# An encoder trunk on one core: the gate's activation table loaded in the last projection, and a down block's weight rounding behind the last pair's evictions

## Chip, cores and metric

The kernel runs on one core of a Trainium2 chip. The metric is the device time of the program in microseconds, the median of several runs. Engines are called as the profile calls them: PE (TensorE), DVE (VectorE), ACT (ScalarE), POOL (GpSimd) and SP (SyncE, which here only issues DMAs).

## Reference

A trunk of two layers over 512 tokens of width 1024, all in float32. Each layer has three token mixers side by side, gates that merge them, a last projection `w_o` with residual, a SwiGLU feed-forward stage of width 2816 and a gated input embedding.

```python
for i in range(DEPTH):                                   # DEPTH = 2
    h = rmsnorm(x, norm_mix[i])
    ...                                                  # three mixers: ya, yb, yc
    ga, gb, gc = jnp.split(jax.nn.sigmoid(gates), 3, axis=-1)
    merged = ga*(ya @ w_br_a[i]) + gb*(yb @ w_br_b[i]) + gc*(yc @ w_br_c[i])
    x = x + merged @ w_o[i]
    h = rmsnorm(x, norm_ffn[i])
    x = x + (jax.nn.silu(h @ w_ffn_gate[i]) * (h @ w_ffn_up[i])) @ w_ffn_down[i]
    h = rmsnorm(x, norm_ple[i])
    x = x + jax.nn.sigmoid(h @ w_ple_gate[i]) * (p[i] @ w_ple_in[i])
return rmsnorm(x, norm_final)
```

## The kernel before

**A product.** Activations stay on chip, transposed (features on the 128 partitions, 512 tokens along the free axis). Every float32 operand is split into a rounded high part and a low remainder, and a product is three matmuls: high·high, high·low, low·high (`mm3`). For weights, SP loads a raw tile `wr` by DMA, ACT rounds it into `wh` (a Copy activation: "the rounding"), and DVE subtracts for `wl` ("the low part"). `wr`, `wh` and `wl` have three buffers each. PSUM has three banks `mm`, two `sc`, two `tr` and one `av`. In traces a tile carries the name of the stage that made it: `ffn_wh`, `wo_x`, `mergeb_wr`.

**The order.** PE executes its matmuls in the order in which the code writes them. The other engines' instructions are placed by a list scheduler, by dependencies and priorities: `high_priority` lifts weight work ahead of what is written around it, and `behind(i, then)` orders instruction `i` after `then` on the same engine without a semaphore. Each engine then runs its queue in order, so an instruction that waits holds all behind it.

**ACT's tables.** ACT holds one set of function tables at a time; a change of set is an instruction of its own, `ACT_TABLE_LOAD`, which the build puts ahead of the first activation that needs another set. `act(..., table=...)` orders activations so that functions of different sets aren't mixed. Both programs hold 13 such loads.

**Stages of a layer.** Mixers, gates, two merge stages (the second, `mergeb`, multiplies by eight blocks of `w_br_b`, one about every 2.7 us), then `w_o`: eight output blocks, each with residual, the operands for the next norm and, in `quarters`, differences of activations t1 to t4 for the feed-forward stage. Then `ffn`, then `ple`.

**The feed-forward stage.** The 22 blocks of 128 gate and up columns are worked off in three parts of 8, 7 and 7 (`PARTS`). For one block, `seven` computes gate and up together as a 2×2 block product with seven instead of eight multiplications (Strassen-Winograd). Its weights are a11, a12 (one `wr` tile), a22 (`kh` and `a`), and the sums s1 to s4: s1, s2 are summed by POOL's accumulating DMAs into `qk` and rounded into `wh`; s3, s4 are summed on DVE into the last `qk` tile and rounded into a spare pair of tiles, `pt` for even blocks and `y` for odd ones. Three PSUM accumulators C, A and Q collect the products: three `mm` banks for an even block, `sc`, `sc`, `av` for an odd one. Evictions (ACT Copy, DVE add) bring them into `t` tiles; PE writes A once more, with s4, after A was evicted for s2. Products with 128x512 operands are L1005 and L1006 (odd blocks), with 128x256 operands L1008 to L1010 (even blocks). `rest`, flushed a little later, applies SiLU on ACT, multiplies by up on DVE and splits the result into a mid. Two blocks are interleaved (`sevens_of`). The s3 sum of each layer's block 2 is placed behind the split of block 0's mid (`self.held`), so block 0's SiLU stands ahead of it.

After each part come eight down blocks, each a sum over the part's mids. The first two run as a `pair`: all mids but the last for both, then the last mid for both, since the last block's SiLU is still to come; then `gemm` for the other six.

The lines of before that matter most are L143 (every activation), L157 (every two-operand DVE instruction), L171 (a weight tile's DMA), L177 to L179 (`mm3`), L908 (the residual's DMA in `w_o`), L1005 to L1010 (`product`). In the changed kernel the lines behind L162 are two higher, those of `seven` three.

Of the kernel before, what the change touches and what calls it, by code (L numbers as in the profile page):

```python
# [14 lines left out]
AF = mybir.ActivationFunctionType  # L15
# [5 lines left out]
P = 128  # L21
# [40 lines left out]
class Net:  # L62
# [96 lines left out]
    def stt(self, out, a, s, b, op0, op1):  # L159
        return self.nc.vector.scalar_tensor_tensor(out, a, s, b, op0, op1)  # L160

    def split(self, hi, lo, src):  # L162
        self.act(hi, src, AF.Copy)
        return self.tt(lo, src, hi.bitcast(F32), ALU.subtract)

    def weights(self, ap, n):
        with self.tc.high_priority(offset=min(self.w_ahead, self.tc.cur_priority - self.p0)):
            raw = self.sb("wr", [P, 1024])
            hi = self.sb("wh", [P, 1024], F32R)
            lo = self.sb("wl", [P, 1024], F32R)  # L170
            self.nc.sync.dma_start(raw[:, :n], ap[:, :n])  # L171
            self.low = self.split(hi[:, :n], lo[:, :n], raw[:, :n])
        return hi, lo

    def mm3(self, out, wh, wl, ah, al, first, last, **kw):
# [15 lines left out]
                         first and o + k == 0, last and o + k == n - 1)  # L191
                self.chunk()

    def pair(self, outs, aps, acts):


        n = len(acts)
        ws = [self.weights(ap, n * P) for ap in aps]
        for ks in (range(n - 1), (n - 1,)):
            for out, (wh, wl) in zip(outs, ws):  # L200
                for k in ks:
                    s = slice(k * P, (k + 1) * P)
                    self.mm3(out, wh[:, s], wl[:, s], *self.halves(acts[k]), k == 0, k == n - 1)
                    self.chunk()
# [695 lines left out]
    def w_o(self, mg, xsrc):  # L900
        self.phase = "wo"
        xs, h, st, self.four = [], [], [], []
        self.zs = [self.parts_of("z", [2, 256], 2, F32R) for _ in range(4)]
        for m in range(KD):
            if m % 2 == 0:
                two = self.parts_of("x", [512], 2)
            xo = two[m % 2]
            self.nc.sync.dma_start(xo, xsrc[m])  # L908
            if m == 0:
                both = [self.ps("mm") for _ in range(2)]  # L910
                self.pair(both, self.a["w_o"][self.i, 0:2], mg)
            if m < 2:
                ps = both[m]
            else:
                ps = self.ps("mm")
                self.gemm(ps, self.a["w_o"][self.i, m], mg)
            self.tt(xo, xo, ps, ALU.add)
            h.append(self.norm_chunk(m, xo, self.par(self.i, "ffn", m), "h", st, 512 if m % 2 else 256))
            xs.append(xo)
            if m == 4:  # L920
                self.mark = self.low_x
            if m in QUARTERS:
                self.four.append(self.quarters(xs, h, QUARTERS.index(m)))
        self.four.append(self.quarters(xs, h, 3))
        self.main_norm(st[0])
        return xs, h
# [31 lines left out]
    def seven(self, wg, wu, bs, tags, spare, md, first, fb, early, twice):  # L958
# [3 lines left out]
        with self.tc.high_priority(offset=min(self.w_ahead, self.tc.cur_priority - self.p0)):  # L962
            lo, up = slice(0, 512), slice(512, 1024)
# [10 lines left out]
            ws = {}  # L974

            def halve(hi, lo, src, names):
                i = self.split(hi, lo, src)
                for q, name in enumerate(names):
                    c = slice(q * 512, q * 512 + 512)
                    ws[name] = (hi[:, c], lo[:, c])  # L980
                return i

            wide = lambda: (self.sb("wh", [P, 1024], F32R), self.sb("wl", [P, 1024], F32R))
            i = halve(*wide(), g, ("a11", "a12"))
# [4 lines left out]
            i = self.tt(s3, s1, a22, ALU.add)  # L989
# [6 lines left out]
        C, A, Q = (self.ps(t, shape) for t in tags)  # L996

        def product(out, w, b, first=False):
            wh, wl = ws[w]
            mm = nc.tensor.matmul  # L1000
            for k in range(4):
                c = slice(k * P, k * P + P)
                both = bs[k][b]
                if len(out.shape) > 2:
                    mm(out, wh[:, c], both, start=first and k == 0, stop=False, skip_group_check=True)  # L1005
                    mm(out[:, 0], wl[:, c], both[:, 0], start=False, stop=k == 3, skip_group_check=True)  # L1006
                    continue
                mm(out, wh[:, c], both[:, 0], start=first and k == 0, stop=False, skip_group_check=True)  # L1008
                mm(out, wh[:, c], both[:, 1], start=False, stop=False, skip_group_check=True)  # L1009
                mm(out, wl[:, c], both[:, 0], start=False, stop=k == 3, skip_group_check=True)  # L1010
            self.chunk2()

        gg, uu = self.sb("t", [P, 2, 256]), self.sb("t", [P, 2, 256])
# [24 lines left out]
        product(A, "s2", "t1")  # L1038
        if twice:
            self.act(uu[:, 1], A[:, 0], AF.Copy)  # L1040
            self.act(gg[:, 0], A[:, 1], AF.Copy)
        else:
            self.act(uu[:, 1], A, AF.Copy)
        product(Q, "a22", "t4")
        if twice:
            self.tt(uu[:, 1], uu[:, 1], gg[:, 0], ALU.add)
# [32 lines left out]
    def sevens_of(self, pairs, head):  # L1079


        def go(*gens):
            for g in gens:
                next(g, None)
# [8 lines left out]
            one = two  # L1093
        go(one, one)

    def behind(self, i, then):

        self.tc.add_manual_dep(
            i.ins, then.ins.name,
            mybir.DependencyInfo(mybir.DependencyClass.NoSync, mybir.DependencyReason.DATA),  # L1100
            reason="order",
        )
# [12 lines left out]
    def ffn(self, h, x):  # L1115
        self.phase = "ffn"
        i = self.i
        self.halfs, self.pending = 0, []
        st, hn, bs = [], [], self.four
        spare = [[self.sb(t, [P, 1024], F32R) for _ in range(2)] for t in ("pt", "y")]  # L1120
        md8 = [self.sb(t, [P, 2, 512], F32R) for t in ["v"] * 3 + ["z"] + ["y"] * 3]
        md8.append(tuple(self.sb("e", [P, 512], F32R) for _ in range(2)))
        self.sums, self.sevens = [t for _ in range(2) for t in self.parts_of("qk", [1024], 2)], 0
        for part in PARTS:
            mids = md8[:len(part)]
            self.sevens_of((self.seven(self.a["w_fg"][i, fb], self.a["w_fu"][i, fb], bs,
                                       (("mm", "mm", "mm"), ("sc", "sc", "av"))[fb % 2],
                                       spare[fb % 2], md8[f], part[0] and f < 2, fb, fb == 0,
                                       fb % 2 == 1)
                            for f, fb in enumerate(part)), part[0] == 0)  # L1130
            self.flush()
            down = [self.a["w_fd"][i, m][:, part[0] * P:(part[-1] + 1) * P] for m in range(KD)]
            two = [self.ps(("mm", "sc")[part[-1] % 2 == 0]) for _ in range(2)]
            self.pair(two, down[:2], mids)
            for m in range(KD):
                if m < 2:
                    ps = two[m]
                else:
                    ps = self.ps("mm")
                    self.gemm(ps, down[m], mids)  # L1140
                d = self.sb("t", [P, 512])
                self.tt(d, ps, self.rb, ALU.mult)
                self.tt(x[m], x[m], d, ALU.subtract)
                if part is PARTS[-1]:
                    if m in (0, 2):
                        qk = self.parts_of("qk", [2, 512], 2, F32R)
                    hn.append(self.norm_chunk(m, x[m], self.par(i, "ple", m),
                                              qk[m % 2] if m < 4 else "z", st))
        self.main_norm(st[0])
        return hn  # L1150
# [109 lines left out]
    def final(self, h, x, pairs, hn, most):  # L1260
# [54 lines left out]
        def store(t):  # L1315
# [11 lines left out]
            nc.sync.dma_start(out[:, c], r[:, c])  # L1327

        pair, low, pgs, vs, columns, summed = [], [], [], [], [], []
        places = ("av", "mm", "av", "sc")  # L1330
        def inputs(t):
# [167 lines left out]
```

## Time and profile before

| | |
|---|---|
| median of 3 runs | 1768.84 us (1768.34 to 1769.42) |
| the profiled execution | 1768.67 us; its span 1766.9 us, 1.8 us lie around it |
| PE busy | 1757.0 us, 99% of the span, 9618 matmuls |
| DVE, ACT busy | 1387.4 us (79%), 934.6 us (53%) |
| granted TensorE clock | 1.0 throughout |
| DMA | 253.90 MB, mean 144 GB/s |

Starts are microseconds from the span's start, and the second number of a timeline row is the duration. Matmuls overlap, so a row's start and the start of the row behind it tell how long PE took, not its duration. The bracket at the end of a row is the engine's idle time ahead of it and the instruction whose end released it. "x2" stands for two instructions in a row of the same kind. The chain of work that ended last is followed back from the last instruction: a row of ACT or DVE in it is a time in which PE waited for that engine. The first layer's feed-forward stage begins at about 490 us, the second's at about 1365.

### The profile page before, as it was taken

What the parts mean: (1) busy time and instruction counts of PE and PEld (TensorE: products, weight loads), DVE (VectorE), ACT (ScalarE), POOL (GpSimd) and SP (SyncE); (2) the same over time, 40 slices, a digit from 0 to 9 for tenths busy, and PEclk for the clock granted to TensorE, in tenths of its full rate; (3) what the DMA queues carried; (4) which work ended last, traced back from release to release, by engine and by line L of the source; (5) the groups of instructions that cost most, each with busy time, mean ns of one, the idle gap of its engine ahead of it and who ended that gap; (6) DMA issues with size and microseconds to landing.
All of it is one profiled execution on the core that took longest, in us unless ns stands there. A gap on an engine that the chain in (4) does not pass through costs nothing.

```text
span 1766.9 us, 26211 instructions
## 1 busy us (share of the span) xinstructions
PE 1757.0 (99%) x9618; PEld 1525.0 (86%) x9618; DVE 1387.4 (79%) x2264; ACT 934.6 (53%) x1647; POOL 103.9 (6%) x114
## 2 busy tenths in 40 slices
PE   9999999999999999999999999999999999999998
PEld 7889888888899898898888888888888998989987
DVE  7967988998788676787776789789887875877776
ACT  5566555325576264464545655552356753645554
POOL 0000000000121010100000000000001210101000
PEclk9999999999999999999999999999999999999999
DMA  6565641334767365543446655322356663655332
GB/s 230 161 191 153 169 116 56 103 103 155 210 162 191 107 169 153 145 123 122 153 133 169 193 142 161 102 77 92 105 188 182 173 173 115 179 143 155 93 105 96
DMA packets 114785, 253.90 MB, mean 144 GB/s; under 512 B 16864, under 2 KB 23776, under 8 KB 114656
## 3 DMA queue, kind: packets, MB, share of 16 engines
q1 hardware_dynamic: 101264, 227.83, 41.9%
q0 software_dynamic: 12672, 23.07, 7.9%
q8 instruction: 76, 1.25, 0.3%
q10 hardware_dynamic: 720, 1.31, 0.2%
q14 instruction: 53, 0.43, 0.1%
HBM read 215.46 MB, written 7.34 MB: 126 GB/s over the span
## 4 chain that ended last, share of the span: by engine, by line
PE 97%; DVE 1%; ACT 1%; issue 0%; DMA 0%; POOL 0%; SPq 0%; ACTq 0%; POOLq 0%; DVEq 0%
PE ffn_sc L1005 6%; PE ffn_mm L177 4%; PE ffn_mm L178 4%; PE ffn_mm L179 4%; PE ffn_mm L1010 3%; PE ffn_mm L1008 3%; PE ffn_mm L1009 3%; PE ffn_sc L1006 3%; PE mergea_mm L178 2%; PE mergea_mm L177 2%; PE mergea_mm L179 2%; PE diff_sc L796 2%; PE diff_mm L177 2%; PE diff_mm L178 2%; PE gatec_mm L178 2%; PE gatec_mm L177 2%
## 5 line engine op out<-in xcount | busy, mean ns | idle before, releaser
L160 DVE SCALAR_TENSOR_TENSOR conv_z<-glu_z,pre_par,conv_z 128x512 f32<-128x512 f32 x240 | 179.7, 749 | 3.4
L143 ACT ACTIVATE ffn_wh<-ffn_wr 128x1024 fp32r<-128x1024 f32 (+1 forms) x92 | 93.3, 1021 | 122.9 <-PE ffn_mm L178 75.8
L157 DVE TENSOR_TENSOR ffn_wl<-ffn_wr,ffn_wh 128x1024 fp32r<-128x1024 f32 (+1 forms) x92 | 107.7, 1176 | 40.0 <-ACT ffn_wh L143 39.5
L973 POOL DMA_DIRECT2D ffn_qk<-w_fu x88 | 77.9, 968 | 600.0 <-DMA ffn_qk<-w_fu 180.7
L157 DVE TENSOR_TENSOR ffn_t<-ffn_mm,wo_rb 128x512 f32<-128x512 f32 (+1 forms) x86 | 48.0, 559 | 61.0 <-PE ffn_mm L179 52.8
L143 ACT ACTIVATE mergea_wh<-mergea_wr 128x1024 fp32r<-128x1024 f32 (+1 forms) x32 | 27.1, 846 | 96.8 <-PE mergea_mm L178 79.6
L157 DVE TENSOR_TENSOR ffn_t<-ffn_t,ffn_t 128x512 f32<-128x512 f32 x88 | 54.6, 620 | 19.0 <-ACT ffn_t L143 19.0
L157 DVE TENSOR_TENSOR ffn_wl<-ffn_qk,ffn_wh 128x1024 fp32r<-128x1024 f32 x44 | 53.9, 1224 | 16.2 <-ACT ffn_wh L143 16.2
L1005 PE MATMUL ffn_sc<-wo_h,ffn_wh 128*128 128x512 f32 x176 | 64.1, 398 | 0.0
L143 ACT ACTIVATE ffn_wh<-ffn_qk 128x1024 fp32r<-128x1024 f32 x44 | 46.6, 1059 | 31.4 <-PE ffn_mm L178 16.1
L143 ACT ACTIVATE diff_a<-diff_sc,diff_s 128x512 f32<-128x512 f32 x32 | 22.0, 688 | 71.2 <-DVE diff_s L889 71.2
L177 PE MATMUL ffn_mm<-ffn_v,ffn_wh 128*128 128x512 f32 x132 | 51.4, 390 | 0.0
L178 PE MATMUL ffn_mm<-ffn_v,ffn_wh 128*128 128x512 f32 x132 | 51.4, 390 | 0.0
L179 PE MATMUL ffn_mm<-ffn_v,ffn_wl 128*128 128x512 f32 x132 | 51.4, 389 | 0.0
L177 PE MATMUL ffn_mm<-ffn_y,ffn_wh 128*128 128x512 f32 x132 | 51.4, 389 | 0.0
L179 PE MATMUL ffn_mm<-ffn_y,ffn_wl 128*128 128x512 f32 x132 | 51.4, 389 | 0.0
L178 PE MATMUL ffn_mm<-ffn_y,ffn_wh 128*128 128x512 f32 x132 | 51.4, 389 | 0.0
L1008 PE MATMUL ffn_mm<-wo_h,ffn_wh 128*128 128x256 f32 x176 | 50.0, 284 | 0.0
L1009 PE MATMUL ffn_mm<-wo_h,ffn_wh 128*128 128x256 f32 x176 | 49.8, 283 | 0.0
L1010 PE MATMUL ffn_mm<-wo_h,ffn_wl 128*128 128x256 f32 x176 | 49.8, 283 | 0.0
L1006 PE MATMUL ffn_sc<-wo_h,ffn_wl 128*128 128x256 f32 x176 | 49.5, 281 | 0.0
L143 ACT ACTIVATE natten_wh<-natten_wr 128x1024 fp32r<-128x1024 f32 x24 | 25.4, 1057 | 42.2 <-issue 15.2
(846 smaller groups left out, 6329.0 us busy)
## 6 DMA issues: line engine op xcount, KB each, us to landing
ffn_qk<-w_fu POOLq DMA_DIRECT2D x88, 256.0 KB, 6.4
ffn_wr<-w_fg SPq DMA_DIRECT2D x44, 512.0 KB, 4.4
ffn_wr<-w_fd SPq DMA_DIRECT2D x32, 448.0 KB, 4.0
ffn_r<-w_fu SPq DMA_DIRECT2D x44, 256.0 KB, 3.4
ffn_qk<-w_fg SPq DMA_DIRECT2D x44, 256.0 KB, 3.1
ffn_qk<-w_fu SPq DMA_DIRECT2D x44, 256.0 KB, 3.3
natten_wr<-w_in SPq DMA_DIRECT2D x16, 512.0 KB, 4.1
diff_wr<-w_in SPq DMA_DIRECT2D x16, 512.0 KB, 4.1
```

Of the source, the lines that this page charges most:

```text
L143: i = self.nc.scalar.activation(out, in_, func, **kw)
L157: return self.nc.vector.tensor_tensor(out, a, b, op)
L160: return self.nc.vector.scalar_tensor_tensor(out, a, s, b, op0, op1)
L177: mm(out, wh, ah, start=first, stop=False, **kw)
L178: mm(out, wh, al, start=False, stop=False, **kw)
L179: mm(out, wl, ah, start=False, stop=last, **kw)
L973: nc.gpsimd.dma_start(q, wu[:, lo], accum_op=ALU.add)
L1005: mm(out, wh[:, c], both, start=first and k == 0, stop=False, skip_group_check=True)
L1006: mm(out[:, 0], wl[:, c], both[:, 0], start=False, stop=k == 3, skip_group_check=True)
L1008: mm(out, wh[:, c], both[:, 0], start=first and k == 0, stop=False, skip_group_check=True)
L1009: mm(out, wh[:, c], both[:, 1], start=False, stop=False, skip_group_check=True)
L1010: mm(out, wl[:, c], both[:, 0], start=False, stop=k == 3, skip_group_check=True)
```

## The change

Two edits.

In `w_o`, after the fifth output block, a new `table` method writes one dummy SiLU of a 128x1 tile of ones into a small tile, with `table="silu"`, so that the set of tables is loaded by it and not by the first SiLU of the feed-forward stage.

`seven` remembers its second-product eviction of A as `self.cleared`; the last block's is handed to `pair`, which hands it to `weights` for its second block, whose rounding `split` places behind that eviction on ACT.

```diff
@@ -159,17 +159,19 @@
     def stt(self, out, a, s, b, op0, op1):
         return self.nc.vector.scalar_tensor_tensor(out, a, s, b, op0, op1)
 
-    def split(self, hi, lo, src):
-        self.act(hi, src, AF.Copy)
+    def split(self, hi, lo, src, then=None):
+        i = self.act(hi, src, AF.Copy)
+        if then is not None:
+            self.behind(i, then)
         return self.tt(lo, src, hi.bitcast(F32), ALU.subtract)
 
-    def weights(self, ap, n):
+    def weights(self, ap, n, then=None):
         with self.tc.high_priority(offset=min(self.w_ahead, self.tc.cur_priority - self.p0)):
             raw = self.sb("wr", [P, 1024])
             hi = self.sb("wh", [P, 1024], F32R)
             lo = self.sb("wl", [P, 1024], F32R)
             self.nc.sync.dma_start(raw[:, :n], ap[:, :n])
-            self.low = self.split(hi[:, :n], lo[:, :n], raw[:, :n])
+            self.low = self.split(hi[:, :n], lo[:, :n], raw[:, :n], then)
         return hi, lo
 
     def mm3(self, out, wh, wl, ah, al, first, last, **kw):
@@ -191,11 +193,11 @@
                          first and o + k == 0, last and o + k == n - 1)
                 self.chunk()
 
-    def pair(self, outs, aps, acts):
+    def pair(self, outs, aps, acts, then=None):
 
 
         n = len(acts)
-        ws = [self.weights(ap, n * P) for ap in aps]
+        ws = [self.weights(ap, n * P, then if k else None) for k, ap in enumerate(aps)]
         for ks in (range(n - 1), (n - 1,)):
             for out, (wh, wl) in zip(outs, ws):
                 for k in ks:
@@ -919,6 +921,7 @@
             xs.append(xo)
             if m == 4:
                 self.mark = self.low_x
+                self.table("silu", AF.Silu)
             if m in QUARTERS:
                 self.four.append(self.quarters(xs, h, QUARTERS.index(m)))
         self.four.append(self.quarters(xs, h, 3))
@@ -1038,9 +1041,9 @@
         product(A, "s2", "t1")
         if twice:
             self.act(uu[:, 1], A[:, 0], AF.Copy)
-            self.act(gg[:, 0], A[:, 1], AF.Copy)
+            self.cleared = self.act(gg[:, 0], A[:, 1], AF.Copy)
         else:
-            self.act(uu[:, 1], A, AF.Copy)
+            self.cleared = self.act(uu[:, 1], A, AF.Copy)
         product(Q, "a22", "t4")
         if twice:
             self.tt(uu[:, 1], uu[:, 1], gg[:, 0], ALU.add)
@@ -1093,6 +1096,10 @@
             one = two
         go(one, one)
 
+    def table(self, name, func):
+
+        self.act(self.sb("s", [P, 1]), self.ones[:, 0:1], func, table=name)
+
     def behind(self, i, then):
 
         self.tc.add_manual_dep(
@@ -1131,7 +1138,7 @@
             self.flush()
             down = [self.a["w_fd"][i, m][:, part[0] * P:(part[-1] + 1) * P] for m in range(KD)]
             two = [self.ps(("mm", "sc")[part[-1] % 2 == 0]) for _ in range(2)]
-            self.pair(two, down[:2], mids)
+            self.pair(two, down[:2], mids, self.cleared)
             for m in range(KD):
                 if m < 2:
                     ps = two[m]
```

PE's and POOL's orders are unchanged. What the scheduler makes of the rest is alike in both layers. In the rows below the middle number is a tile's buffer; the changed kernel's are one higher from the dummy on.

ACT in the merge stage, before: the rounding of the fourth `mergeb` block stands behind a feed-forward rounding.

```order
L143 ACTIVATE pin_kh_785_4340<-pin_t_784_4339 128x512
L143 ACTIVATE ffn_kh_889_4791<-ffn_r_886_4780 128x512
L143 ACTIVATE mergeb_wh_761_4221<-mergeb_wr_760_4220 128x512
L143 ACTIVATE mergeb_y_748_4168<-gatec_x_333_1921 128x512
L143 ACTIVATE mergeb_wh_766_4245<-mergeb_wr_765_4244 128x512
```

The same place in the changed kernel, where `wo_s` is the dummy's tile:

```order
L143 ACTIVATE pin_kh_785_4340<-pin_t_784_4339 128x512
L143 ACTIVATE ffn_kh_890_4793<-ffn_r_887_4782 128x512
L143 ACT_TABLE_LOAD
L143 ACTIVATE wo_s_831_4568<-pre_ones_31_106 128x1
L143 ACTIVATE mergeb_wh_761_4221<-mergeb_wr_760_4220 128x512
L143 ACTIVATE mergeb_y_748_4168<-gatec_x_333_1921 128x512
L143 ACTIVATE mergeb_wh_766_4245<-mergeb_wr_765_4244 128x512
```

The load and the dummy now stand ahead of that fourth rounding, earlier than the fifth output block of `w_o` in whose code they are written.

DVE at the first blocks, before: `ffn_wl_927` is the low part of block 2's s1, s2; `ffn_qk_884<-...,ffn_r_921` its s3 and `ffn_qk_884<-...,ffn_wr_920` its s4, `ffn_pt_871` the low part of both; `ffn_wl_937` and `ffn_a_939` are low parts of block 3, the last row is block 3's s3.

```order
L157 TENSOR_TENSOR ffn_wl_927_5012<-ffn_qk_884_4778,ffn_wh_926_5011 128x1024
L157 TENSOR_TENSOR ffn_v_874_4768<-ffn_t_896_4806,ffn_v_874_4768 128x512
L157 TENSOR_TENSOR ffn_qk_884_4778<-ffn_qk_884_4778,ffn_r_921_4996 128x512
L157 TENSOR_TENSOR ffn_wl_937_5125<-ffn_wr_934_5116,ffn_wh_936_5124 128x1024
L157 TENSOR_TENSOR ffn_qk_884_4778<-ffn_qk_884_4778,ffn_wr_920_4995 128x512
L157 TENSOR_TENSOR ffn_a_939_5129<-ffn_r_935_5117,ffn_kh_938_5128 128x512
L157 TENSOR_TENSOR ffn_t_916_4913<-ffn_t_916_4913,ffn_t_915_4912 128x256
L157 TENSOR_TENSOR ffn_t_916_4913<-ffn_av_914_4911,ffn_t_916_4913 128x256
L157 TENSOR_TENSOR ffn_pt_871_4765<-ffn_qk_884_4778,ffn_pt_870_4764 128x1024
L157 TENSOR_TENSOR ffn_t_916_4913<-ffn_t_916_4913,ffn_t_915_4912 128x512
L157 TENSOR_TENSOR ffn_qk_884_4778<-ffn_qk_883_4777,ffn_r_935_5117 128x512
```

And in the changed kernel:

```order
L157 TENSOR_TENSOR ffn_wl_928_5014<-ffn_qk_885_4780,ffn_wh_927_5013 128x1024
L157 TENSOR_TENSOR ffn_v_875_4770<-ffn_t_897_4808,ffn_v_875_4770 128x512
L157 TENSOR_TENSOR ffn_qk_885_4780<-ffn_qk_885_4780,ffn_r_922_4998 128x512
L157 TENSOR_TENSOR ffn_qk_885_4780<-ffn_qk_885_4780,ffn_wr_921_4997 128x512
L157 TENSOR_TENSOR ffn_wl_938_5127<-ffn_wr_935_5118,ffn_wh_937_5126 128x1024
L157 TENSOR_TENSOR ffn_t_917_4915<-ffn_t_917_4915,ffn_t_916_4914 128x256
L157 TENSOR_TENSOR ffn_pt_872_4767<-ffn_qk_885_4780,ffn_pt_871_4766 128x1024
L157 TENSOR_TENSOR ffn_a_940_5131<-ffn_r_936_5119,ffn_kh_939_5130 128x512
L157 TENSOR_TENSOR ffn_qk_885_4780<-ffn_qk_884_4779,ffn_r_936_5119 128x512
L157 TENSOR_TENSOR ffn_t_917_4915<-ffn_av_915_4913,ffn_t_917_4915 128x256
L157 TENSOR_TENSOR ffn_qk_885_4780<-ffn_qk_885_4780,ffn_wr_935_5118 128x512
L157 TENSOR_TENSOR ffn_t_917_4915<-ffn_t_917_4915,ffn_t_916_4914 128x512
```

Block 2's s4 now stands ahead of block 3's first low part, and `ffn_pt` ahead of `ffn_a` and of the eviction that reads `ffn_av`; block 3's s3 stands ahead of that eviction too.

ACT at the same place, before, from the load and the first SiLU (`ffn_t_896<-ffn_t_896`) to the rounding of block 2's s3, s4 (`ffn_pt_870`):

```order
L143 ACT_TABLE_LOAD
L143 ACTIVATE ffn_t_896_4806<-ffn_t_896_4806 128x512
L143 ACTIVATE ffn_wh_926_5011<-ffn_qk_884_4778 128x1024
L143 ACTIVATE ffn_v_874_4768<-ffn_t_896_4806 128x512
L143 ACTIVATE ffn_mm_929_5020<-ffn_mm_928_5019 128x256
L143 ACTIVATE ffn_wh_936_5124<-ffn_wr_934_5116 128x1024
L143 ACTIVATE ffn_t_916_4913<-ffn_sc_913_4910 128x256
L143 ACTIVATE ffn_t_915_4912<-ffn_sc_913_4910 128x256
L143 ACTIVATE ffn_kh_938_5128<-ffn_r_935_5117 128x512
L143 ACTIVATE ffn_t_916_4913<-ffn_av_914_4911 128x256
L143 ACTIVATE ffn_t_932_5023<-ffn_tr_933_5059 128x256
L143 ACTIVATE ffn_pt_870_4764<-ffn_qk_884_4778 128x1024
```

In the changed kernel:

```order
L143 ACTIVATE ffn_t_897_4808<-ffn_t_897_4808 128x512
L143 ACTIVATE ffn_wh_927_5013<-ffn_qk_885_4780 128x1024
L143 ACTIVATE ffn_v_875_4770<-ffn_t_897_4808 128x512
L143 ACTIVATE ffn_mm_930_5022<-ffn_mm_929_5021 128x256
L143 ACTIVATE ffn_wh_937_5126<-ffn_wr_935_5118 128x1024
L143 ACTIVATE ffn_t_917_4915<-ffn_sc_914_4912 128x256
L143 ACTIVATE ffn_t_916_4914<-ffn_sc_914_4912 128x256
L143 ACTIVATE ffn_pt_871_4766<-ffn_qk_885_4780 128x1024
L143 ACTIVATE ffn_kh_939_5130<-ffn_r_936_5119 128x512
L143 ACTIVATE ffn_t_917_4915<-ffn_av_915_4913 128x256
L143 ACTIVATE ffn_t_933_5025<-ffn_tr_934_5061 128x256
```

The load is gone, and `ffn_pt` stands ahead of `ffn_kh` and of two evictions.

ACT at the end of the first part, before: the roundings of the second (`ffn_wh_1010`) and third (`ffn_wh_1016`) down blocks stand around the last block's `ffn_y_880` and ahead of the two evictions of its A bank, `ffn_t_1002` and `ffn_t_1001`.

```order
L143 ACTIVATE ffn_t_987_5490<-ffn_t_987_5490 128x512
L143 ACTIVATE ffn_wh_1010_5745<-ffn_wr_1009_5744 128x1024
L143 ACTIVATE ffn_y_880_4774<-ffn_t_987_5490 128x512
L143 ACTIVATE ffn_wh_1016_5806<-ffn_wr_1015_5805 128x1024
L143 ACTIVATE ffn_t_1002_5612<-ffn_sc_999_5609 128x256
L143 ACTIVATE ffn_t_1001_5611<-ffn_sc_999_5609 128x256
L143 ACTIVATE ffn_kh_1062_6102<-ffn_r_1059_6091 128x512
```

In the changed kernel:

```order
L143 ACTIVATE ffn_t_988_5492<-ffn_t_988_5492 128x512
L143 ACTIVATE ffn_y_881_4776<-ffn_t_988_5492 128x512
L143 ACTIVATE ffn_t_1003_5614<-ffn_sc_1000_5611 128x256
L143 ACTIVATE ffn_t_1002_5613<-ffn_sc_1000_5611 128x256
L143 ACTIVATE ffn_wh_1011_5747<-ffn_wr_1010_5746 128x1024
L143 ACTIVATE ffn_wh_1017_5808<-ffn_wr_1016_5807 128x1024
L143 ACTIVATE ffn_kh_1063_6104<-ffn_r_1060_6093 128x512
```

Both roundings moved behind both evictions, though only the second block's is named in the code; at the ends of the second and third parts they move in the same way. The `kh` rounding behind them belongs to the next part.

On SP, one of the two residual loads `wo_x` that stood behind the first `w_o` weight tile now stands ahead of it, and one load of a late `w_fd` tile stands one place later.

## Prediction

> **What bounds the kernel.** I read the page first, then the chain of work that ended last in order of time, then the gaps between the starts of matmuls on the timeline.
>
> ```profile
> span 1766.9 us, 26211 instructions
> PE 97%; DVE 1%; ACT 1%; issue 0%; DMA 0%; POOL 0%; SPq 0%; ACTq 0%; POOLq 0%; DVEq 0%
> ```
>
> ```profile
> 506.54 1.28 ACT L143
> ...
> 571.15 0.64 ACT ffn_t L143 x2
> ...
> 1381.91 1.28 ACT L143
> ```
>
> PE carries 97% of the chain, and the change touches no matmul, so it can win only time in which PE stands still. In mid-program the chain leaves PE at few places, all in the feed-forward stage and alike in both layers (506.54 and 1381.91 are the same table load, one layer apart): at the first blocks, and at the ends of the first and third parts. PE's own starts give their size.
>
> At the first blocks, PE is about to use block 2's s3/s4 weights (`ffn_pt`):
>
> ```profile
> 514.11 0.28 PE L1006 MATMUL ffn_sc<-wo_h,ffn_y 128*128 128x256 f32 x1
> 514.75 0.39 PE L1008 MATMUL ffn_mm<-wo_rp,ffn_pt 128*128 128x256 f32 x1 [0.36 <-ACT ffn_pt L143]
> ...
> 516.29 0.28 PE L1008 MATMUL ffn_mm<-wo_rp,ffn_pt 128*128 128x256 f32 x1
> ...
> 518.69 0.28 PE L1010 MATMUL ffn_mm<-wo_h,ffn_wl 128*128 128x256 f32 x1
> 518.81 0.40 PE L1005 MATMUL ffn_sc<-wo_h,ffn_wh 128*128 128x512 f32 x1
> ```
>
> Half-width matmuls start 0.12 us apart (518.69 to 518.81). Unhindered, the three that follow 514.11 would start at 514.23, 514.35 and 514.47, and the next at 514.59; that one starts at 516.29. PE loses **1.70 us** here, waiting first for the high part (from ACT), then for the low part (from DVE).
>
> At the part ends, PE wants to write the last block's A bank again and waits until ACT has copied it out (the chain's 571.15 row):
>
> ```profile
> 570.98 0.28 PE L1006 MATMUL ffn_av<-wo_z,ffn_a 128*128 128x256 f32 x1
> ...
> 571.34 0.28 PE L1006 MATMUL ffn_av<-wo_z,ffn_a 128*128 128x256 f32 x1
> ...
> 572.17 0.27 PE L1006 MATMUL ffn_sc<-wo_h,ffn_y 128*128 128x256 f32 x1
> ```
>
> ```profile
> 793.00 0.28 PE L1006 MATMUL ffn_av<-wo_z,ffn_a 128*128 128x256 f32 x1
> ...
> 793.72 0.28 PE L1006 MATMUL ffn_sc<-wo_h,ffn_y 128*128 128x256 f32 x1
> ```
>
> The even step is 0.36 (570.98 to 571.34). Part 1 takes 0.83, so it loses **0.47**; part 3 takes 0.72 and loses **0.36**. The second part's last block is an even one and shows no such gap. Ceiling of the whole change: 2 layers × (1.70 + 0.47 + 0.36) = 5.06 us, or 0.29% of the run.
>
> **The load, taken out of the first blocks.** ACT and DVE there:
>
> ```profile
> 506.54 1.28 ACT L143 ACT_TABLE_LOAD   x1
> 507.83 0.63 ACT L143 ACTIVATE ffn_t<-ffn_t 128x512 f32<-128x512 f32 x1
> 508.37 1.04 ACT L143 ACTIVATE ffn_wh<-ffn_qk 128x1024 fp32r<-128x1024 f32 x1
> ...
> 510.14 1.06 ACT L143 ACTIVATE ffn_wh<-ffn_wr 128x1024 fp32r<-128x1024 f32 x1
> ...
> 511.62 0.63 ACT L143 ACTIVATE ffn_kh<-ffn_r 128x512 fp32r<-128x512 f32 x1
> ...
> 513.64 1.06 ACT L143 ACTIVATE ffn_pt<-ffn_qk 128x1024 fp32r<-128x1024 f32 x1 [0.24 <-DVE ffn_qk L157]
> ```
>
> ```profile
> 509.44 1.23 DVE L157 TENSOR_TENSOR ffn_wl<-ffn_qk,ffn_wh 128x1024 fp32r<-128x1024 f32 x1 [0.26 <-ACT ffn_wh L143]
> 510.58 0.68 DVE L157 TENSOR_TENSOR ffn_v<-ffn_t,ffn_v 128x512 fp32r<-128x512 f32 x1
> 511.19 0.69 DVE L157 TENSOR_TENSOR ffn_qk<-ffn_qk,ffn_r 128x512 f32<-128x512 f32 x1
> ...
> 512.92 0.69 DVE L157 TENSOR_TENSOR ffn_qk<-ffn_qk,ffn_wr 128x512 f32<-128x512 f32 x1
> ...
> 514.79 1.22 DVE L157 TENSOR_TENSOR ffn_pt<-ffn_qk,ffn_pt 128x1024 fp32r<-128x1024 f32 x1
> ...
> 517.13 0.42 DVE L157 TENSOR_TENSOR ffn_t<-ffn_sc,ffn_t 128x256 f32<-128x256 f32 x1
> ```
>
> Without the load SiLU starts at 506.54, 1.29 earlier. The next rounding, 508.37, can't follow by the whole 1.29: its buffer is still read by PE.
>
> ```profile
> 506.80 0.40 PE L1005 MATMUL ffn_sc<-wo_h,ffn_wh 128*128 128x512 f32 x1
> 507.03 0.28 PE L1006 MATMUL ffn_sc<-wo_h,ffn_wl 128*128 128x256 f32 x1
> ```
>
> The first row ends at 507.20; with a tenth for the signal the rounding starts at 507.30, 1.07 earlier. DVE then follows its changed order with the steps above (1.14 after a whole low part, 0.61 and 0.60 after half-size ones): low part 508.37, `ffn_v` 509.51, s3 510.12, and s4 now directly behind it at 510.72, not 512.92. The low part that s4 overtakes goes to 511.32; its own rounding stays at 510.14, since PE releases that buffer. ACT's slot for the high part of `ffn_pt` is now where `ffn_kh` stood, 511.62, and s4 (0.72 from its start to the rounding, 512.92 to 513.64) is ready at 511.44; so high part 511.62 to 512.68, low part 512.79 to 514.01. PE wants them at 514.23 and 514.47. The wait is gone, with 0.46 us to spare: **1.70** won.
>
> What is late next: the moved instructions (block 3's low part `ffn_a`, an eviction of the av bank, block 3's s3) stand behind `ffn_pt` on DVE, and the eviction that frees block 2's sc bank follows them. By the same steps it starts at 516.67 instead of 517.13 and ends at 517.09; PE wants the bank at 518.81 − 1.70 = 517.11. With 0.06 for the signal that is a tie. I charge **0.15** a layer; the bounds are 0 and, if DVE runs as late as it does now (517.13 + 0.42 = 517.55), 0.5.
>
> **The load, put into the merge stage.** There it costs itself and the dummy, for which the program's start has a row:
>
> ```profile
> 2.47 0.20 ACT L143 ACTIVATE pre_rc<-pre_ones 128x1 f32<-128x1 f32 x1
> ...
> 425.20 0.63 ACT L143 ACTIVATE mergeb_wh<-mergeb_wr 128x512 fp32r<-128x512 f32 x1
> ```
>
> ```profile
> 429.31 0.68 DVE L157 TENSOR_TENSOR mergeb_wl<-mergeb_wr,mergeb_wh 128x512 fp32r<-128x512 f32 x1
> ```
>
> So 1.28 + 0.20 = 1.48: the rounding at 425.20 moves to about 426.7 and ends at 427.3. DVE doesn't read it before 429.31, as it is busy with earlier merge work: 2 us of cover. Cost 0; were the cover gone, 1.5 a layer. The set that SiLU loads also serves the Copy and Square that run until then, so no load is added (13 in both programs). SP now issues one of two residual loads ahead of the first `w_o` tile:
>
> ```profile
> 432.74 0.80 SPq L908 DMA_DIRECT2D wo_x<-xT  x2
> ```
>
> That is half of 0.80, so this tile comes 0.4 later; PE uses it only after the remaining merge blocks, more than that away. Cost 0.
>
> The Trainium skill ("ScalarE: Activation LUTs", What ACT_TABLE_LOAD costs) gives some 2.66 us for each switch of sets, the load and a drain behind it. The rows show no drain: SiLU starts 0.01 us after the load ends. By the page's figure the load and the dummy would overdraw the merge stage's cover by 2.66 + 0.20 − 2.0 = 0.86 us a layer, and the sum would be 1765.8.
>
> **The down blocks' rounding.** Part 1's end on ACT, and when PE is done with A:
>
> ```profile
> 568.71 1.06 ACT L143 ACTIVATE ffn_wh<-ffn_wr 128x1024 fp32r<-128x1024 f32 x1 [0.18 <-PE ffn_sc L1005]
> ...
> 570.20 1.05 ACT L143 ACTIVATE ffn_wh<-ffn_wr 128x1024 fp32r<-128x1024 f32 x1
> ```
>
> ```profile
> 569.93 0.28 PE L1006 MATMUL ffn_sc<-wo_z,ffn_wl 128*128 128x256 f32 x1
> ...
> 573.33 0.39 PE L177 MATMUL ffn_mm<-ffn_v,ffn_wh 128*128 128x512 f32 x1
> ```
>
> A is complete at 570.21, but ACT holds the third block's rounding until 571.15. With both roundings behind them the two copies run from about 570.25 to 570.9, ahead of 571.46, when PE would like to write: **0.47** won. Part 3 has the same order, and its copies end about 0.6 ahead: **0.36** won. Part 2 has nothing to win. The moved roundings come up to 2.1 later (568.71 to about 570.85). The second block's is done by 571.9 and its low part, 1.2 long on DVE, by about 573.2. PE needs them after the first block's seven ready mids, three matmuls each at the full-width step of 0.23 (506.80 to 507.03): 573.33 + 21 × 0.23 − 0.47 = 577.7. Cost 0, with 4 us of cover.
>
> What is queued behind: the raw tiles come free up to 2.1 late, and SP with them.
>
> ```profile
> 563.95 9.18 SPq L171 DMA_DIRECT2D ffn_wr<-w_fd x3
> ```
>
> ```profile
> ffn_wr<-w_fd SPq DMA_DIRECT2D x32, 448.0 KB, 4.0
> ```
>
> ```profile
> 583.53 2.01 ACT L143 ACTIVATE ffn_wh<-ffn_wr 128x1024 fp32r<-128x1024 f32 x2 [4.57 <-PE ffn_mm L178]
> ```
>
> The third tile is issued by 573.13 and lands about 577.1, and ACT rounds it at 583.53, when PE frees a buffer: 6.4 us of cover against 2.1. Cost 0.
>
> **Sum.** 2 × (1.70 − 0.15 + 0.47 + 0.36) = 4.76 us. The profiled execution took 1768.67 us, the median of the runs is 1768.84; from the median, **1764.1 us** (0.27% less). A difference under 0.2% (3.5 us, below 1765.3 or above 1772.4) can hardly be told from no change here.
>
> **Rivals.**
> 1. Only part of the first blocks' wait goes. For it: `ffn_pt` hangs on a chain of six instructions on two engines, each placed by hand above, and DVE is full there. If the low part of `ffn_pt` comes no earlier than the first low part does, that is 1.07, PE still loses 0.63 there. If s4 in effect still waits for the low part that it overtakes, which can't start before its rounding ends (510.14 + 1.06, about 511.29, where before it started 1.13 ahead of the row of 512.92, at 511.79), only 0.50 is won. With 0.83 from the part ends that is 2 × 1.90 = 3.80 to 2 × 1.33 = 2.66: 1765.0 to 1766.2, **1765.6** in the middle. Against it: s4 stands ahead in the changed order, with 0.46 to spare. Chance 0.16.
> 2. A load costs wherever it stands, and only the down half works: 2 × 0.83 = 1.66, **1767.2**. It would need ACT's delay in the merge stage to reach PE with as much as the first blocks win; the 2 us of cover speak against it. The Trainium skill's rule (same page and section) that every switch of sets has its price points this way, as the count of switches stays. Chance 0.05.
> 3. Slower: the late raw tiles arrive on PE's path. Six part ends (three in each layer) at up to 2.1 each are 12.6 if nothing covers them: 1764.1 + 12.6 = **1776.7**. It ends above 1772.4 only if each is exposed by 1.4, that is if less than 0.7 of the 6.4 us of cover is real. Chance 0.04.
> 4. All of the ceiling, the sc bank's tie won: **1763.8**. Chance 0.06; with the forecast's own 0.69 this is the same mechanism.
>
> The range 1763.2 to 1766.3 runs from the ceiling, less 0.6 for the spread of runs (1768.34 to 1769.42), to rival 1's far end. Left out are rivals 2 and 3 and the ends of the others, about 0.15. Faster by over 0.2%: the forecast (0.69), rival 4 and a third of rival 1, less 0.03 for a forecast that ends just short: 0.77. The same: those 0.03, the rest of rival 1 and rival 2, 0.19 with what rounding leaves. Slower: 0.04.
>
> **What would show it.** Right: no load ahead of the first SiLU of a layer's feed-forward; the first L1008, L1009 and L1010 on `ffn_pt` of block 2 start 0.12 apart each, and the L1006 at a part end 0.36 after the one before it; a load in the merge stage with PE's `mergeb` matmuls as even as before. Wrong: a wait at L1010 with DVE as its releaser (rival 1), a new gap in the merge stage or at `w_o`'s first product (rival 2), gaps in the down blocks with a DMA as releaser (rival 3).

## The result, and the profile after

The changed kernel takes 1764.62 us, the median of 10 runs (1763.70 to 1765.81); the kernel before, run beside it, takes 1768.77 (1768.02 to 1769.55). The ratio is 0.9976, 95% interval 0.9968 to 0.9984: faster by 0.24%, or 4.15 us, where 4.76 were forecast. The profiled execution's span went from 1766.9 to 1763.1 us.

The page of the changed kernel, the lines on the span and on the shares of the chain of work that ended last:

```profile
span 1763.1 us, 26202 instructions
PE 99%; DVE 0%; ACT 0%; POOL 0%; issue 0%; POOLq 0%; ACTq 0%; DVEq 0%
```

The chain no longer leaves PE in mid-program: in order of time, its rows for other engines lie in the first 1.1 us and behind 1746.8 us, in the last layer's end.

Where the time came from is best read matmul by matmul. PE executes the same 9618 matmuls in the same order in both programs, so the start of each can be set against that of its counterpart; where the difference jumps, a wait has gone or come. (The traces of this document also differ by up to 0.8 us in the first 10 us, and by up to 0.7 in each layer's attention, at about 180 and 1050 us, where the orders of PE, ACT, DVE and POOL are the same; why, no run shows, and these jumps are left out.) In the first layer the jumps are −1.69 at the first `ffn_pt` products, +0.26 at 517.86, +0.27 at 523.79, −0.49 at the end of part 1 and −0.39 at the end of part 3, −2.04 in all; in the second −1.70, +0.24, +0.27, −0.48 and −0.39, −2.06. That is 4.1 us, and the medians show 4.15.

The three waits that went: in the changed kernel the lines of `product` are three higher (L1011 to L1013 for L1008 to L1010, L1008 and L1009 for L1005 and L1006). PE's timeline at the first use of `ffn_pt`:

```profile
514.67 0.28 PE L1009 MATMUL ffn_sc<-wo_h,ffn_y 128*128 128x256 f32 x1
514.79 0.28 PE L1011 MATMUL ffn_mm<-wo_rp,ffn_pt 128*128 128x256 f32 x1
...
515.15 0.28 PE L1011 MATMUL ffn_mm<-wo_rp,ffn_pt 128*128 128x256 f32 x1
```

From the first to the last of these 0.48 us pass, four even steps of 0.12; before it was 2.18 (514.11 to 516.29). At the ends of parts 1 and 3:

```profile
570.72 0.28 PE L1009 MATMUL ffn_av<-wo_z,ffn_a 128*128 128x256 f32 x1
...
571.07 0.28 PE L1009 MATMUL ffn_sc<-wo_h,ffn_y 128*128 128x256 f32 x1
```

```profile
791.88 0.28 PE L1009 MATMUL ffn_av<-wo_z,ffn_a 128*128 128x256 f32 x1
...
792.22 0.28 PE L1009 MATMUL ffn_sc<-wo_h,ffn_y 128*128 128x256 f32 x1
```

0.35 and 0.34 where 0.83 and 0.72 passed. Two waits came. Both are so short that the rows name no releaser; only the steps show them (0.31 and 0.29 where 0.12 is even):

```profile
517.55 0.28 PE L1013 MATMUL ffn_mm<-wo_h,ffn_wl 128*128 128x256 f32 x1
517.86 0.47 PE L1008 MATMUL ffn_sc<-wo_h,ffn_wh 128*128 128x512 f32 x1
...
523.50 0.28 PE L1013 MATMUL ffn_tr<-wo_z,ffn_wl 128*128 128x256 f32 x1
523.79 0.39 PE L1011 MATMUL ffn_mm<-wo_h,ffn_pt 128*128 128x256 f32 x1
```

What ended just before them, on DVE and on ACT:

```profile
517.29 0.42 DVE L157 TENSOR_TENSOR ffn_t<-ffn_sc,ffn_t 128x256 f32<-128x256 f32 x1
```

```profile
520.86 1.06 ACT L143 ACTIVATE ffn_wh<-ffn_wr 128x1024 fp32r<-128x1024 f32 x1 [1.77 <-PE ffn_mm L1012]
521.82 0.58 ACT L143 ACTIVATE ffn_sc<-ffn_sc 128x512 f32<-128x512 f32 x1
522.34 0.61 ACT L143 ACTIVATE ffn_t<-ffn_t 128x512 f32<-128x512 f32 x1
522.85 0.62 ACT L143 ACTIVATE ffn_kh<-ffn_r 128x512 fp32r<-128x512 f32 x1
523.38 0.36 ACT L143 ACTIVATE ffn_t<-ffn_mm 128x256 f32<-128x256 f32 x1
```

The first is the eviction that frees a C bank for block 3. The last copies out block 2's A bank, which PE then writes again with s4; in the changed kernel block 1's SiLU and block 4's `kh` rounding stand ahead of it. Before, `kh` stood behind it, and PE's step there was even (0.12, from 524.38 to 524.50):

```profile
522.71 0.36 ACT L143 ACTIVATE ffn_t<-ffn_mm 128x256 f32<-128x256 f32 x1
...
523.49 0.62 ACT L143 ACTIVATE ffn_kh<-ffn_r 128x512 fp32r<-128x512 f32 x1
```

In the merge stage ACT shows the load where the order put it:

```profile
425.73 1.28 ACT L143 ACT_TABLE_LOAD   x1
427.03 0.20 ACT L143 ACTIVATE wo_s<-pre_ones 128x1 f32<-128x1 f32 x1
427.14 0.62 ACT L143 ACTIVATE mergeb_wh<-mergeb_wr 128x512 fp32r<-128x512 f32 x1
```

1.41 us from the start of the load to the rounding behind it, and no jump in PE's starts anywhere in this stage.

### The profile page after: what moved, and what is told of

Read it like the earlier page. It is cut to its first block, busy times and chain, and to the rows that moved or that the text cites. A ratio compares the mean times of both kernels' runs of the same rounds, so it can differ in the third digit from the quotient of the medians.

```text
span 1763.1 us, 26202 instructions
## 1 busy us (share of the span) xinstructions
PE 1756.3 (100%) x9618; PEld 1525.2 (87%) x9618; DVE 1388.2 (79%) x2264; ACT 934.6 (53%) x1649; POOL 104.1 (6%) x114
## 4 chain that ended last, share of the span: by engine, by line
PE 99%; DVE 0%; ACT 0%; POOL 0%; issue 0%; POOLq 0%; ACTq 0%; DVEq 0%
PE ffn_sc L1008 6%; PE ffn_mm L179 4%; PE ffn_mm L180 4%; PE ffn_mm L181 4%; PE ffn_mm L1011 4%; PE ffn_mm L1013 4%; PE ffn_mm L1012 4%; PE ffn_sc L1009 3%; PE mergea_mm L179 2%; PE mergea_mm L181 2%; PE mergea_mm L180 2%; PE diff_sc L798 2%; PE diff_mm L179 2%; PE diff_mm L180 2%; PE gatec_mm L180 2%; PE natten_mm L180 2%
## 5 line engine op out<-in xcount | busy, mean ns | idle before, releaser
L1008 PE MATMUL ffn_sc<-wo_h,ffn_wh 128*128 128x512 f32 x176 | 64.2, 399 | 0.1
L1011 PE MATMUL ffn_mm<-wo_h,ffn_wh 128*128 128x256 f32 x176 | 50.0, 284 | 0.0
L1013 PE MATMUL ffn_mm<-wo_h,ffn_wl 128*128 128x256 f32 x176 | 49.8, 283 | 0.0
L1009 PE MATMUL ffn_sc<-wo_h,ffn_wl 128*128 128x256 f32 x176 | 49.5, 281 | 0.0
```

## The experiments

Times are medians, with the kernel before run beside them on the same chip (1768.7 to 1769.1).

**Each edit alone.** The first without the second:

```diff
-            self.pair(two, down[:2], mids, self.cleared)
+            self.pair(two, down[:2], mids)
```

> Edit 1 alone: the dummy SiLU in w_o, the down blocks as before. Theory (the change's gain is the sum of PE waits that are independent of one another): at the first blocks 1.69 won, 0.24 lost at the sc bank and 0.28 at the s4 product of block 2, so 2 x 1.17 = 2.3 us less than before, about 1766.4; the waits at the part ends (0.47 and 0.36) stay. Rival (the down blocks' placement matters only together with the moved load, or the gain is all the load's): as the changed kernel, 1764.6.

Measured: 1766.05 (ratio 0.9985, 0.9976 to 0.9994), 2.6 us less than before. PE's jumps are −1.69, +0.23 and +0.27 in the first layer and −1.70, +0.24 and +0.29 in the second, and nothing at the part ends.

The second without the first:

```diff
-                self.table("silu", AF.Silu)
```

> Edit 2 alone: the second down block's rounding behind the evictions, no dummy. Theory: the two part ends of each layer lose their waits, 2 x (0.48 + 0.39) = 1.7 us less than before, about 1767.0, and the first blocks wait 1.70 as before. Rival (the late raw tiles cost): no gain, or slower than before by up to 2 us a part end.

Measured: 1767.00 (0.9990, 0.9981 to 0.9999), 1.7 us less. The only jumps are −0.49, −0.38, −0.48 and −0.38 at the four part ends. The two gains add up (2.6 + 1.7 = 4.3 against 4.15): they are separate waits, and the late raw tiles of rival 3 cost nothing.

**The load's own time, or the order it leaves?** In the forecast the 1.70 needed two things: the load away and s4 ahead of the low part that it overtakes. Here the load is away, and one order edge holds s4 back:

```diff
             if fb == 1:
                 self.behind(i, self.held)
+            if fb == 3:
+                self.behind(self.s4, i)
...
-            self.tt(s4, s3, g[:, up], ALU.add)
+            self.s4 = self.tt(s4, s3, g[:, up], ALU.add)
```

With this edge both engines stand at the first blocks as they stood before, less the load. Only one eviction on ACT (`ffn_t<-ffn_tr`) stands behind the rounding of `ffn_pt` instead of ahead of it, and that rounding waits for DVE there.

> Both edits, but block 2's s4 sum is ordered behind the low part of block 3's first weights, as it stood before; with that, ACT and DVE at the first blocks stand in the order of before, without the load. It separates the load's 1.28 us from the order that its absence brings. Theory (the load alone shifts the chain little, since the low part ahead of s4 waits for a rounding that PE releases): ffn_pt comes 0.50 earlier instead of 1.69, no new wait at the sc bank or at the s4 product; with the part ends 2 x (0.50 + 0.87) = 2.7 less than before, about 1766.0. Rival (it is the load's own time that counts): 1.28 or more a layer from the first blocks, 2 x (1.28 + 0.87) = 4.3 less, 1764.5 or below.

Measured: 1765.98 (0.9984, 0.9975 to 0.9993). PE wins 0.57 and 0.55 at `ffn_pt`, and neither of the two new waits appears. ACT and DVE show what holds the chain:

```profile
510.90 1.06 ACT L143 ACTIVATE ffn_wh<-ffn_wr 128x1024 fp32r<-128x1024 f32 x1 [0.98 <-PE ffn_sc L1010]
```

```profile
511.99 1.23 DVE L157 TENSOR_TENSOR ffn_wl<-ffn_wr,ffn_wh 128x1024 fp32r<-128x1024 f32 x1 [0.48 <-ACT ffn_wh L143]
513.14 0.68 DVE L157 TENSOR_TENSOR ffn_qk<-ffn_qk,ffn_wr 128x512 f32<-128x512 f32 x1
...
515.01 1.21 DVE L157 TENSOR_TENSOR ffn_pt<-ffn_qk,ffn_pt 128x1024 fp32r<-128x1024 f32 x1
```

ACT waits 0.98 for PE to free a buffer, DVE waits 0.48 for ACT's rounding, and s4 stands behind. Of the load's 1.28 us less than 0.6 arrive at PE; the other 1.1 of the 1.69 come from s4's new place. This is the far end of rival 1 (0.50) as a kernel of its own.

The other way round, the load kept and s4 put ahead:

```diff
             if fb == 1:
                 self.behind(i, self.held)
+            if fb == 3:
+                self.behind(i, self.s4)
```

> The kernel before, with its load ahead of the first SiLU and its down blocks, but block 3's first rounding's low part ordered behind block 2's s4 sum, as in the changed kernel. Theory (order and load are worth little apart): by the steps of DVE s4 goes to about 512.1 and the low part of ffn_pt to 514.5 instead of 514.8, 0.3 earlier, and the s4 product of block 2 may wait 0.28 as in the changed kernel: 0 to 0.6 us less than before, 1768.2 to 1768.8. Rival (the order does it all): 2 x 1.17 less or more, 1766.4 or below.

Measured: 1770.03 (1.0006, 0.9998 to 1.0015), 1.3 more than before where 0 to 0.6 less was expected. The interval still holds 1, so what was lost is read from the trace. The gain at `ffn_pt` came as worked out, 0.33 and 0.34 net, but the one edge moved other rows too, two blocks on. PE and DVE there:

```profile
539.07 0.28 PE L1012 MATMUL ffn_mm<-wo_h,ffn_wl 128*128 128x256 f32 x1
539.84 0.47 PE L1007 MATMUL ffn_sc<-wo_h,ffn_wh 128*128 128x512 f32 x1 [0.49 <-DVE ffn_t L157]
```

```profile
538.14 1.22 DVE L157 TENSOR_TENSOR ffn_y<-ffn_qk,ffn_y 128x1024 fp32r<-128x1024 f32 x1
539.28 0.75 DVE L157 TENSOR_TENSOR ffn_t<-ffn_sc,ffn_t 128x256 f32<-128x256 f32 x2
```

The eviction of a C bank now stands behind a 1.14 us low part that it preceded in the kernel before, and PE loses 0.78 a layer, 0.72 of it at this place: 2 × (0.78 − 0.33) = 0.9 of the 1.3; the rest is within the spread of runs. So neither the load's place nor the order gives the gain alone.

**The two new waits.** Block 4's `kh` rounding is put behind the eviction of block 2's A bank:

```diff
-            def halve(hi, lo, src, names):
-                i = self.split(hi, lo, src)
+            def halve(hi, lo, src, names, then=None):
+                i = self.split(hi, lo, src, then)
...
-            low = halve(self.sb("kh", [P, 512], F32R), self.sb("a", [P, 512], F32R), a22, ("a22",))
+            low = halve(self.sb("kh", [P, 512], F32R), self.sb("a", [P, 512], F32R), a22, ("a22",),
+                        self.cleared if fb == 4 else None)
```

> The changed kernel, with the rounding of block 4's a22 (kh) placed behind the first eviction of block 2's A bank on ACT. Theory: in the changed kernel PE starts the s4 product of block 2 0.28 late in each layer, because that eviction (523.38) stands behind the kh rounding (522.85); with 0.52 less ahead of it the wait is gone: 2 x 0.28 = 0.56 less than the changed kernel, about 1764.1. Rival (SiLU ahead of it, or the end of the product before it, sets the eviction's time): the wait stays, 1764.6.

Measured: 1763.51 (0.9969, 0.9958 to 0.9980). Against the changed kernel's trace PE's only jumps in the feed-forward stage are −0.27 and −0.26 at these products; the medians' 1.1 is more than these 0.53, and what is beyond lies within the spread of runs.

In addition, block 3's s4 is put behind the eviction that frees the C bank:

```diff
-            self.tt(s4, s3, g[:, up], ALU.add)
+            i = self.tt(s4, s3, g[:, up], ALU.add)
+            if fb == 3:
+                self.behind(i, self.freed)
...
             for n, o in enumerate((C, A)):
                 self.act(gg[:, n], o[:, 1], AF.Copy)
-                self.tt(gg[:, n], o[:, 0], gg[:, n], ALU.add)
+                i = self.tt(gg[:, n], o[:, 0], gg[:, n], ALU.add)
+                if n == 0:
+                    self.freed = i
```

> As the run before it, and block 3's s4 sum on DVE placed behind the eviction of block 1's C bank, so that this bank is free earlier. Theory: the wait of 0.2 to 0.25 in each layer at the first product of block 3's second accumulation (517.86) goes too: 2 x (0.28 + 0.24) = 1.0 less than the changed kernel, about 1763.6, which is the ceiling that the prediction worked out. Rival (block 3's s3 and s4 are on the path, and come late): a new wait at the y weights of block 3, no gain or a loss.

Measured: 1763.52 (0.9969, 0.9956 to 0.9981); the span is 1761.8. PE at both places:

```profile
517.37 0.28 PE L1016 MATMUL ffn_mm<-wo_h,ffn_wl 128*128 128x256 f32 x1
517.49 0.40 PE L1011 MATMUL ffn_sc<-wo_h,ffn_wh 128*128 128x512 f32 x1
...
523.06 0.28 PE L1016 MATMUL ffn_tr<-wo_z,ffn_wl 128*128 128x256 f32 x1
523.18 0.28 PE L1014 MATMUL ffn_mm<-wo_h,ffn_pt 128*128 128x256 f32 x1
```

Even steps of 0.12. The jumps against the changed kernel's trace are −0.26 at the bank and −0.27 at the s4 product in either layer, 1.06 together; the medians differ by 1.1. Both causes hold, and the kernel stands at the ceiling that the prediction set 5.06 us below the kernel before (5.6 below the one run beside it, 5.25 below the median of the first comparison). The medians of these two kernels are alike, so they don't show what the second edge is worth; its 0.26 a layer is shown by the starts in the traces alone.

**What a load costs where it is covered.** One more switch of tables in each merge stage, a dummy Exp ahead of the dummy SiLU:

```diff
+                self.table("exp", AF.Exp)
                 self.table("silu", AF.Silu)
```

> The changed kernel with one more switch of tables in each layer's merge stage: a dummy Exp ahead of the dummy SiLU, so two loads and two dummies there. Theory (a load costs only what the stage doesn't cover; ACT has about 1.5 us idle in each merge block's 2.72, a load with its dummy takes 1.4): no cost that can be seen, PE's mergeb matmuls even, 1764.6 with at most 0.2 a layer. Rival (every switch has its price): 1.28 a layer and up, 1767.2; by the Trainium skill (ScalarE: Activation LUTs, What ACT_TABLE_LOAD costs), with 2.66 for each switch, 1769.9.

Measured: 1764.90 (0.9976, 0.9966 to 0.9985), no jump at the merge blocks. The same two lines twice, so three more switches a layer:

> The changed kernel with three more switches in each layer's merge stage (Exp, SiLU, Exp, SiLU dummies), which stand between four successive roundings of the merge blocks. Theory (cover): each load falls into another block's idle 1.5 us of ACT, so 0 to 0.5 a layer, 1764.6 to 1765.6; where it begins to cost, DVE's low parts start late and PE shows gaps at mergeb. Rival (every switch has its price): 3 x 1.28 x 2 = 7.7 more, 1772.3, or by the Trainium skill's 2.66 (same page and section) 16 more, 1780.6.

Measured: 1764.55 (0.9975, 0.9965 to 0.9985), no jump. ACT there:

```profile
427.69 1.28 ACT L143 ACT_TABLE_LOAD   x1
428.99 0.20 ACT L143 ACTIVATE wo_s<-pre_ones 128x1 f32<-128x1 f32 x1
429.10 0.62 ACT L143 ACTIVATE mergeb_wh<-mergeb_wr 128x512 fp32r<-128x512 f32 x1
429.62 0.61 ACT L143 ACTIVATE mergeb_y<-gatec_x 128x512 fp32r<-128x512 f32 x1
430.25 1.28 ACT L143 ACT_TABLE_LOAD   x1
```

A load and its dummy fill the gap that ACT has in each block of 2.72 us: eight loads in the two merge stages instead of two, for nothing. To find where the cover ends, the loads are put together, all ahead of the fourth merge block's rounding (`self.fourth`, noted in `merge_b`):

```diff
-                self.table("silu", AF.Silu)
+                for _ in range(1):          # 2 in the second of these kernels
+                    self.table("exp", AF.Exp)
+                    d = self.table("silu", AF.Silu)
+                self.behind(self.fourth, d)
```

> The changed kernel with two switches in each layer, one behind the other, both ahead of the fourth merge block's rounding (2 x 1.41 us instead of one). Theory (cover): in the changed kernel that rounding runs from 427.14 and PE reads the high part at 431.18 and the low part at 431.63; 1.41 later it is still 2 us early: no cost, 1764.6. Rival (every switch has its price): 1764.6 + 2 x 1.28 = 1767.2 or more.

Measured: 1764.74 (0.9977, 0.9967 to 0.9987), no jump. On ACT 2.91 us pass from the first load to the rounding, 1.50 more than the 1.41 of the changed kernel:

```profile
425.28 1.28 ACT L143 ACT_TABLE_LOAD   x1
...
428.19 1.14 ACT L143 ACTIVATE mergeb_wh<-mergeb_wr 128x512 fp32r<-128x512 f32 x2
```

> The same with four switches ahead of that rounding. Theory (cover, and now it is gone): three more loads and dummies are 4.2 us, and one 0.6 us activation stands between them, so the rounding runs from about 432.0 to 432.6 and its low part from 432.7 to 433.4; PE starts the fourth merge block at 432.6 instead of 431.2 and its first low part product 1.75 late: 2 x 1.75 = 3.5 more than the changed kernel, about 1768.1. Rival (cover is larger than the rows show): no cost, 1764.6; rival (every switch has its price): 3 x 1.28 x 2 = 7.7 more, 1772.3.

Measured: 1768.93 (1.0005, 0.9996 to 1.0015), 4.3 more than the changed kernel (4.2 more than the kernel with two, run beside it) where 3.5 was expected. Its ten executions spread from 1768.15 to 1771.56; the trace is of one of 1768.46. ACT's rounding and PE's wait for it:

```profile
425.42 1.28 ACT L143 ACT_TABLE_LOAD   x1
...
431.87 1.66 ACT L143 ACTIVATE mergeb_wh<-mergeb_wr 128x512 fp32r<-128x512 f32 x3
```

```profile
430.64 0.39 PE L181 MATMUL mergeb_mm<-conv_qk,mergeb_wl 128*128 128x512 f32 x1
432.53 0.50 PE L179 MATMUL mergeb_mm<-conv_qk,mergeb_wh 128*128 128x512 f32 x1 [1.51 <-ACT mergeb_wh L143]
432.87 0.40 PE L180 MATMUL mergeb_mm<-conv_qk,mergeb_wh 128*128 128x512 f32 x1
433.26 0.50 PE L181 MATMUL mergeb_mm<-conv_qk,mergeb_wl 128*128 128x512 f32 x1
```

The rounding comes 6.45 after the first load's start, 5.0 more than in the changed kernel. This trace runs 0.30 ahead of the changed kernel's up to here, so 431.87 is 432.17 on that one's time, where 432.0 was worked out. PE loses 2.05 a layer, not 1.75. So the cover holds one further load (1.5) and not three with the activation between them (5.0). In the changed kernel the low part is ready at 428.48 (427.79 and 0.69 of its own) and PE reads it at 431.63, 3.15 later: of the 5.0 some 1.9 stick out, near the 2.05 that PE lost. That is one kernel; three loads were not run.

## Why the prediction was right

The forecast was 1764.1, the result 1764.62; 0.61 of the 4.76 are missing.

- **The chain that ends in `ffn_pt`.** Ahead of the feed-forward stage the changed kernel's trace runs 0.55 us later than that of before. With that added, s4 was worked out for 511.27 and stands at 511.34, the low part of `ffn_pt` for 513.34 and stands at 513.42. The 1.70 came as 1.69 and 1.70. The instinct to subtract the load's 1.28 from PE's path would have been wrong on both sides: the load alone is worth under 0.6, with the order 1.7.
- **The tie at the sc bank** was the 0.15 a layer; it measured 0.25. The eviction came at 517.29 (517.22 worked out), and PE's matmul 0.15 after its end, not 0.06. The text also named the wrong owner: the bank is C of block 1, an odd block, not of block 2; the place and the time were meant as they are.
- **"What is late next" stopped too early.** This is the step that failed: after the sc bank I looked no further, and 6 us later ACT's changed order (`kh` ahead of the eviction of block 2's A bank; with `kh` alone put back, the wait was gone) cost 0.27 a layer. The sum had no term for it. With both sizes right, 2 × (1.70 − 0.25 − 0.27 + 0.47 + 0.36) = 4.02, against 4.15 measured. The order of ACT at that place could be read beforehand; it was not among the rows looked at.
- **The part ends** were sized 0.47 and 0.36 and gave 0.48 to 0.49 and 0.38 to 0.39. The moved roundings cost nothing, as forecast.

SP's rows of the changed kernel at the end of part 1, the landing of its tiles (128x1024, so 512 KB) and ACT's rounding of the later ones:

```profile
563.33 10.66 SPq L173 DMA_DIRECT2D ffn_wr<-w_fd  x3
```

```profile
ffn_wr<-w_fd SPq DMA_DIRECT2D x16, 512.0 KB, 4.7
```

```profile
582.44 2.01 ACT L143 ACTIVATE ffn_wh<-ffn_wr 128x1024 fp32r<-128x1024 f32 x2 [3.22 <-PE ffn_mm L180]
```

The last of the three issues ends at 573.99, before at 573.13; PE stands 0.61 us earlier here than in the trace of before, so the tiles come 1.5 later for it. With 4.7 for the landing (the 4.0 of the prediction is the median of the 448 KB tiles of the later parts) there are still 3.8 us of cover: ACT waits 3.22 for PE there, not for the tile.

- **The merge stage** cost nothing, as forecast, but the reason given was wrong, and the zero was right by luck. I took 2 us of cover from DVE's row of 429.31, and that row belongs to the fifth block, rounded at 428.46. DVE read the fourth block's rounding (425.20 to 425.83) at 425.88, so on DVE there was no cover at all:

```profile
428.46 0.62 ACT L143 ACTIVATE mergeb_wh<-mergeb_wr 128x512 fp32r<-128x512 f32 x1
```

```profile
425.88 0.68 DVE L157 TENSOR_TENSOR mergeb_wl<-mergeb_wr,mergeb_wh 128x512 fp32r<-128x512 f32 x1
```

The load did delay both, to 427.14 and 427.79 in the changed kernel. What counts is when PE reads the fourth block, its high part at 431.18 and its low part at 431.63:

```profile
427.79 0.69 DVE L157 TENSOR_TENSOR mergeb_wl<-mergeb_wr,mergeb_wh 128x512 fp32r<-128x512 f32 x1
```

```profile
431.18 0.39 PE L179 MATMUL mergeb_mm<-conv_qk,mergeb_wh 128*128 128x512 f32 x1
431.40 0.39 PE L180 MATMUL mergeb_mm<-conv_qk,mergeb_wh 128*128 128x512 f32 x1
431.63 0.39 PE L181 MATMUL mergeb_mm<-conv_qk,mergeb_wl 128*128 128x512 f32 x1
```

Before, PE read the low part at 431.07, 4.5 us after it was ready (426.56). That is the cover, not 2.0, and the 0.86 us by which the prediction saw it overdrawn falls with it. The runs with more loads show where it ends.

- **Rival 2**, and the rule of the Trainium skill ("ScalarE: Activation LUTs", What ACT_TABLE_LOAD costs) that every switch takes some 2.66 us with its drain: the trace doesn't agree. From the start of a load to the activation behind its dummy 1.41 us pass, a drain shows on neither side of it, and six more switches cost nothing that can be measured.

## What to carry to other kernels

When an instruction of a microsecond is taken off a queue, what arrives at the bound engine depends on who else releases each link of the chain: here under 0.6 of 1.28 came through, and another 1.1 only since the scheduler then put one sum ahead of a wait. Where a list scheduler sets the order, an edit's effect does not end at its place: follow every queue whose rows changed to the point where the order is the old one again, and ask of each bank that PE writes twice what now stands ahead of its eviction. A fixed cost such as a table load belongs where its engine has a gap in every step, and its price there is not its length but what sticks out beyond the moment at which the bound engine reads what stands behind it.

## What the runs showed that I had not expected

- After a wait PE's next step is longer, by some 0.1 us: in the kernel with four loads together a step takes 0.34 where 0.23 is even, from 432.53 to 432.87 and from 433.26 to 433.60 (the next row), and in the changed kernel the half-width step behind 523.79 takes 0.22 where 0.12 is even. If that holds for every wait, two short ones cost more than one of their length together; no run sets the two side by side.
- The waits of 0.2 us are named by no row's bracket, and the chain of work that ended last stays at 99% PE. Starts, set against the other program's, show them, and 1 us of this kernel was made of four such.
